# Two transformer blocks on one core: table work dealt by a rate over the feed-forward layers, its stores on GpSimd's queue, relu squares on ScalarE

## The chip, the cores and the metric

The kernel runs on one core of a Trainium2 chip. Its engines are TensorE (PE in the profile: matmuls and transposes), VectorE (DVE), ScalarE (ACT), GpSimd (POOL) and SyncE (SP, which here only issues DMAs). Each engine works through its own list of instructions in order and waits on semaphores for the others. The metric is the device time of one execution in microseconds (us), lower is better. A change of less than about 0.3% is not told from none here.

## The reference

The input is 256 tokens of 1024 features, in fp32. A first block of two layers and a second block of two layers follow one another; each ends in a feed-forward part of the same kind, so there are four of them:

```python
def squared_relu_mlp(h, w1, w2):
    a = jax.nn.relu(h @ w1)
    return (a * a) @ w2
# first block, layer l: x = x + rmsnorm(squared_relu_mlp(rmsnorm(x, g[4]), w_ff1[l], w_ff2[l]), g[5])
# second block, layer i: h = h + squared_relu_mlp_2(rms_norm(h, norm_ffn[i]), ffn_w_up[i], ffn_w_down[i])
```

w1 is 1024 x 4096, w2 4096 x 1024. The second layer of the second block has a state space mixer with weights of its own, of which much can be computed before the mixer's input is known:

```python
lam = lax.complex(a_re, a_im); dt = jnp.exp(log_dt)[..., None]
a_bar = jnp.exp(lam * dt)
b_bar = ((a_bar - 1.0) / lam)[..., None] * b_mat
# per direction r: bu = b_bar[r] u;  states by a scan with a_bar[r];  y = Re(c_mat[r] states)
# 64 groups of 16 features, 64 complex states each, both directions summed
```

## The kernel before

*Matrix products.* fp32 weights are split into two parts, and each product is three matmuls: high by high, low by high, high by low (`mm_a`, L217 to L219, and `mm_b`, L224 to L226). `Seg._load` (L33 on) loads a weight piece into a buffer `raw` (L42, issued by SP, four buffers), ACT makes the high part `whi` (L47, or L53 with a gain), DVE the low part `wlo` (L49 or L58). Ten buffers hold each of the two parts.

*The feed-forward part* (`mlp`, L275). The 4096 middle features are cut into eight chunks of 512. Chunks 0 and 1 are made token-major (`ff1_a`, then `out_a` with the transposes `fftp` of L337), chunks 2 to 7 feature-major (`ff1_b`, `out_b`). Behind the first product of chunk n comes the second product (`ff2`, tile `ffacc`) of chunk n - 2; at the end both last chunks follow with first all of one token half t = 0 and then t = 1. The middle result goes through `relu_sq`: ACT's relu out of the PSUM bank (L298), DVE's square in place (L299); `split` makes its parts `ah` on ACT (L292) and `al` on DVE (L293).

*The end of a feed-forward part.* `residual` (L178) takes the mean square by ACT (`junk`, L168), the factor `r` by DVE and POOL (L170, L171), and DVE adds into X (L200). `feat_half` transposes X on PE (`tp`, L140) and splits it again into `hh` (ACT, L143) and `hl` (DVE, L144) for the next part.

*The side work.* A generator `fill` is advanced one section by each `step(1)`: one at the start, then after each of the 4 column groups of a chunk and after each of the 4 row groups of `ff2`, so 1 + 6 x 8 = 49 steps; `step(100)` runs what is left. The first part (ff0) has `ssm_scalars` for it, 8 sections; the second (ff1) the tables of group blocks 0 to 7, the third (ffb0) those of 8 to 15 and then the loads of `ssm_prefetch`; the fourth (ffb1) has none. A layer's tables are 35 sections.

*A block of tables* (`ssm_tables`, L1354). `first(k)` loads `bc`, `pk`, `gb` and makes the complex products `er` and `gr`, each of four products, two on DVE and two (`cmt`) on POOL (`cmul`, L1149 to L1157), and POOL sets parts of `bm` to zero (L1378, L1379). `second(k)` follows one block later: twice four transposes of er on PE (`etp`, L1402) with a copy `eo` on ACT (L1403), then the lag products `klag` on PE (L1410, L1414), a copy `kl` on ACT (L1416) and a correction on DVE (L1417). What comes out is stored to DRAM tables: d_g, d_e (two halves), d_kl; at the end of the eight blocks d_ks is copied out of d_kl in two DMAs, and d_tt out of d_ks in eight (L1440). All of these DMAs are issued by SP, as the weight loads are.

*Order.* The order of the instructions on each engine is made by a scheduler before the run from the program's order, priorities and dependences; `first` stands at a lower priority. `order` rows below show what came of it.

Of the kernel before, what the change touches and what calls it, by code (L numbers as in the profile page):

```python
# [68 lines left out]
class Core:  # L69
# [204 lines left out]

    def mlp(self, pool, w1, gain, w2, done, perm=False, fill=None):  # L275

# [4 lines left out]
        rsq = []  # L281

        def step(n):
            for _ in range(n):
                if fill is not None:
                    next(fill, None)

# [7 lines left out]
        def relu_sq(ps, view=None):  # L295
            r = pool.tile([128, 512], F32, tag="relu", name="relu", bufs=2)
            o = r if view is None else view(r)
            nc.scalar.activation(out=o, in_=ps if view is None else ps.rearrange("p (f c j) -> p f c j", f=2, j=8), func=AF.Relu)  # L298
            nc.vector.tensor_tensor(out=r, in0=r, in1=r, op=ALU.mult)  # L299
            return r  # L300
# [82 lines left out]
        for ch in range(2, NCH):  # L383
            ps = ff1_b(ch, rest if ch == 2 else None)
            ff2([ch - 2], parts)
            parts[ch] = out_b(ps)
        step(100)
        ff2([NCH - 2, NCH - 1], parts)
# [739 lines left out]
class Ssm:  # L1128
# [225 lines left out]
    def ssm_tables(self, blocks, bc4, gain, d_rows, dmask):  # L1354
# [6 lines left out]
        with self.tc.tile_pool(name="tab", bufs=1, reuse_waits="tile") as pool:  # L1361

            def first(k):
# [24 lines left out]
                with self.low(90):  # L1388
                    gr = pool.tile([128, 4, 2, 8, 16], F32, tag="gr", name="gr", bufs=2)
                    self.cmul(pool, gr[:, :, 0], gr[:, :, 1], pj(16), pj(24), vi(cr), vi(ci), neg_i=True, tag="cte", second=G)  # L1390
                    A.activation(out=ci, in_=ci, func=AF.Copy, scale=-1.0)
                    nc.sync.dma_start(out=self.d_g[k], in_=gr.rearrange("p g r a b -> p (g r a b)"))
                yield k, bc, bm, er, gr

            def second(k, bc, bm, er, gr):
                cr, ci = bc[:, :, 2], bc[:, :, 3]
                for g2 in range(2):
# [5 lines left out]
                    A.activation(out=eo.rearrange("p g r n -> p (g r) n"), in_=ps, func=AF.Copy)  # L1403
                    nc.sync.dma_start(out=self.d_e[k, :, g2 * 512:g2 * 512 + 512], in_=eo.rearrange("p g r n -> p (g r n)"))
                    yield
# [11 lines left out]
                V.scalar_tensor_tensor(out=kl[:, 0:16], in0=dmask, scalar=d_rows[:, k:k + 1], in1=kl[:, 0:16], op0=MU, op1=AD)  # L1417
                nc.sync.dma_start(out=self.d_kl[k], in_=kl)

# [13 lines left out]
            ks = self.d_ks.rearrange("(a q) i n -> a q i n", q=4)  # L1433
            nc.sync.dma_start(out=ks[a0:a1, :, :, 112:240], in_=kl5[a0:a1, :, 0, :, 0:128])
            nc.sync.dma_start(out=ks[a0:a1, :, :, 0:112], in_=kl5[a0:a1, :, 1, :, 32:144])
            yield
            n = 4 * (a1 - a0)
            for r in range(8):
                src = bass.AP(self.d_ks.tensor, self.d_ks.offset + 4 * a0 * 16 * 240 + r * 16, [[240, 16], [3840, n], [1, 128]])
                nc.sync.dma_start(out=self.d_tt[r * 16:r * 16 + 16, 4 * a0:4 * a1, :], in_=src)  # L1440
            yield
# [278 lines left out]
def first_block(c, A):  # L1720
    tc, nc = c.tc, c.nc
    for l in range(2):
# [38 lines left out]
        with tc.tile_pool(name=f"ff{l}", bufs=1, reuse_waits="tile") as pool:  # L1761
            if l == 1:
                c.later.append(lambda: reorder(c))
            c.mlp(pool, A["w_ff1"][l], gc[2], A["w_ff2"][l], lambda t, a, q: c.residual(t, a, post, q), perm=l == 1,
                  fill=tables(c, A, range(8)) if l == 1 else c.ssm_scalars(A["ssm_a_re_2"], A["ssm_a_im_2"], A["ssm_log_dt_2"], c.sgn))

# [20 lines left out]
def second_block(c, A, out):  # L1787
# [5 lines left out]
    with tc.tile_pool(name="ffb0", bufs=1, reuse_waits="tile") as pool:  # L1793
        c.mlp(pool, A["ffn_w_up_2"][0], c.gcols[:, 8, :], A["ffn_w_down_2"][0], lambda t, a, q: c.residual(t, a, None, q, feat=False),
              fill=tables(c, A, range(8, 16), last=True))
    with tc.tile_pool(name="ssm", bufs=1, reuse_waits="tile") as pool:
# [84 lines left out]
```

## Time and profile before

| | us |
|---|---|
| median of three runs | 1510.27 (1508.42 to 1512.3) |
| the profiled execution | 1508.71 |
| its span, first to last instruction | 1506.9 |
| PE busy | 1426.2 |
| DVE busy | 1129.7 |
| ACT busy | 835.0 |
| POOL busy | 184.0 |

The mean granted TensorE clock is 0.979 of full speed. In the rows below a timeline line gives start and duration in us, engine, line, operation, output and inputs, and in brackets the idle time of the engine before it and what ended that; a line of a window gives its bounds, its length, then the busy time of PE, PEld (weight loads of PE), DVE, ACT and POOL with the number of instructions, the granted clock, the share of the DMA engines, and GB/s. SPq is SP's issue of a DMA. The four feed-forward parts lie at about 233.6 to 423.5 (ff0), 646.4 to 869.1 (ff1), 995.4 to 1208.8 (ffb0) and 1313.6 to 1497.0 (ffb1).

### The profile page before, as it was taken

The numbers are of one execution on the slowest core, as the hardware profiler recorded it, in microseconds if no ns is written. First come the engines' busy times: TensorE is split into PE (matmuls) and PEld (weight loads), VectorE is DVE, ScalarE is ACT, GpSimd is POOL, SyncE is SP. The second block draws the span as 40 slices with busy tenths as digits, with TensorE's granted clock in tenths as the row PEclk, the third lists the DMA queues.
The fourth block names the chain that finished last, engine by engine and source line by source line (L and its number), as shares of the span: only waits on it lengthen the run. The fifth ranks groups of instructions, "written<-read, shape, count | busy, mean of one in ns | idle before, by whom it ended". The sixth has DMA issues, their size and how long they took to land. (4 is left out here: it accounts for less than half of the span.)

```text
span 1506.9 us, 25499 instructions
## 1 busy us (share of the span) xinstructions
PE 1426.2 (95%) x9668; PEld 1239.6 (82%) x9668; DVE 1129.7 (75%) x2013; ACT 835.0 (55%) x1432; POOL 184.0 (12%) x206
## 2 busy tenths in 40 slices
PE   8999999999999999989899999999999968999997
PEld 8897888998789798869778877888879756889895
DVE  7986658997776866579995699899995587674651
ACT  7475546454464665556445667665454555564540
POOL 1241001000000000023440010123430000000000
PEclk9999999999999999999999999999999998999999
DMA  8464535475785455365768663347668887655640
GB/s 298 145 206 155 188 119 188 152 238 181 241 284 188 127 182 194 114 210 191 232 211 255 210 219 114 111 146 235 220 223 265 319 315 274 198 184 192 206 158 28
DMA packets 134034, 298.26 MB, mean 198 GB/s; under 512 B 16152, under 2 KB 36376, under 8 KB 133272
## 3 DMA queue, kind: packets, MB, share of 16 engines
q1 hardware_dynamic: 133624, 294.54, 58.9%
q0 software_dynamic: 288, 2.10, 0.4%
q8 instruction: 76, 1.25, 0.3%
q14 instruction: 46, 0.38, 0.1%
HBM read 270.15 MB, written 31.62 MB: 200 GB/s over the span
## 5 line engine op out<-in xcount | busy, mean ns | idle before, releaser
L58 DVE SCALAR_TENSOR_TENSOR wlo<-raw,gcols,whi 128x512 fp32r<-128x512 f32 (+1 forms) x456 | 356.7, 825 | 66.5 <-ACT whi L53 66.3
L53 ACT ACTIVATE whi<-raw,gcols 128x512 fp32r<-128x512 f32 (+1 forms) x456 | 316.7, 745 | 128.0 <-DMA raw<-in_w_ff 27.4
L49 DVE TENSOR_TENSOR wlo<-raw,whi 128x1024 fp32r<-128x1024 f32 x172 | 206.7, 1220 | 65.1 <-ACT whi L47 64.6
L47 ACT ACTIVATE whi<-raw 128x1024 fp32r<-128x1024 f32 x176 | 181.8, 1054 | 99.1 <-DMA raw<-in_ffn_w_down 28.6
L224 PE MATMUL ffps<-hh,whi 128*128 128x256 f32 x768 | 222.0, 289 | 0.2 <-ACT kl L1416 0.2
L226 PE MATMUL ffps<-hl,whi 128*128 128x256 f32 x768 | 219.6, 286 | 0.0
L225 PE MATMUL ffps<-hh,wlo 128*128 128x256 f32 x768 | 219.4, 286 | 0.0
L217 PE MATMUL ffacc<-whi,ah 128*128 128x512 f32 x512 | 206.1, 403 | 2.3 <-ACT whi L47 2.3
L218 PE MATMUL ffacc<-wlo,ah 128*128 128x512 f32 x512 | 203.5, 397 | 0.7 <-DVE wlo L49 0.7
L219 PE MATMUL ffacc<-whi,al 128*128 128x512 f32 x512 | 203.4, 397 | 0.0
L224 PEld LDWEIGHTS ffps<-hh,whi 128*128 128x128 f32 x768 | 148.2, 193 | 2.4 <-issue 1.4
L225 PEld LDWEIGHTS ffps<-hh,wlo 128*128 128x128 f32 x768 | 147.8, 192 | 0.5
L226 PEld LDWEIGHTS ffps<-hl,whi 128*128 128x128 f32 x768 | 147.6, 192 | 0.0
L217 PEld LDWEIGHTS ffacc<-whi,ah 128*128 128x128 f32 x512 | 97.3, 190 | 25.5 <-ACT whi L47 2.7
L218 PEld LDWEIGHTS ffacc<-wlo,ah 128*128 128x128 f32 x512 | 97.5, 190 | 22.7 <-DVE wlo L49 1.6
L219 PEld LDWEIGHTS ffacc<-whi,al 128*128 128x128 f32 x512 | 97.2, 190 | 23.0
L225 PE MATMUL pb<-hh,wlo 128*128 128x256 f32 x352 | 101.1, 289 | 2.9 <-DVE wlo L58 2.9
L224 PE MATMUL pb<-hh,whi 128*128 128x256 f32 x352 | 101.3, 290 | 2.2 <-ACT whi L53 2.2
L226 PE MATMUL pb<-hl,whi 128*128 128x256 f32 x352 | 100.8, 287 | 0.0
L171 POOL TENSOR_TENSOR r<-r,mhalf 128x1 f32<-128x1 f32 x32 | 24.7, 771 | 563.9 <-DVE r L170 557.2
L299 DVE TENSOR_TENSOR relu<-relu 128x512 f32<-128x512 f32 x64 | 45.7, 714 | 58.2 <-ACT relu L298 58.0
L298 ACT ACTIVATE relu<-ffps 128x512 f32<-128x512 f32 x64 | 43.9, 685 | 76.0 <-PE ffps L226 61.6
(481 smaller groups left out, 3001.7 us busy)
## 6 DMA issues: line engine op xcount, KB each, us to landing
raw<-in_w_ff SPq DMA_DIRECT2D x128, 512.0 KB, 4.6
raw<-in_ffn_w_up SPq DMA_DIRECT2D x64, 512.0 KB, 4.5
raw<-in_ffn_w_down SPq DMA_DIRECT2D x64, 512.0 KB, 4.4
raw<-in_w_mem_kv SPq DMA_DIRECT2D x32, 512.0 KB, 4.8
raw<-in_w_qkv SPq DMA_DIRECT2D x24, 512.0 KB, 4.9
raw<-in_attn_w_qkv SPq DMA_DIRECT2D x24, 512.0 KB, 4.7
raw<-in_w_in_ab SPq DMA_DIRECT2D x20, 512.0 KB, 5.1
raw<-in_w_mem_q SPq DMA_DIRECT2D x16, 512.0 KB, 5.1
```

The source lines that it names most:

```text
L47: nc.scalar.activation(out=hi, in_=src, func=AF.Copy)
L49: eng.tensor_tensor(out=lo, in0=src, in1=hi.bitcast(F32), op=ALU.subtract)
L53: nc.scalar.activation(out=hi[:, a], in_=src[:, a], func=AF.Copy, scale=g)
L58: nc.vector.scalar_tensor_tensor(out=lo[:, a], in0=src[:, a], scalar=g, in1=hi[:, a].bitcast(F32), op0=ALU.mult, op1=ALU.subtract)
L217: nc.tensor.matmul(o, xh, wh[:, s], start=first, stop=False)
L218: nc.tensor.matmul(o, xh, wl[:, s], start=False, stop=False)
L219: nc.tensor.matmul(o, xl, wh[:, s], start=False, stop=last)
L224: nc.tensor.matmul(out, wh, xh, start=first, stop=False)
L225: nc.tensor.matmul(out, wl, xh, start=False, stop=False)
L226: nc.tensor.matmul(out, wh, xl, start=False, stop=last)
L298: nc.scalar.activation(out=o, in_=ps if view is None else ps.rearrange("p (f c j) -> p f c j", f=2, j=8), func=AF.Relu)
L299: nc.vector.tensor_tensor(out=r, in0=r, in1=r, op=ALU.mult)
```

## The change

Three things. `step` collects a due count by a rate and advances the side work when it reaches one: 0.2 in ff0, 0.7 in ff1, 0.85 in ffb0. The stores of the tables (d_g, d_e, d_kl, d_ks, d_tt) are issued on GpSimd's queue. In the three parts with side work the square is an ACT instruction.

```diff
@@ -272,7 +272,8 @@
                     self.mm_b(ps[:, f, :], wh[:, c:c + 128], wl[:, c:c + 128], hh[:, :, kt, :], hl[:, :, kt, :], kt == 0, kt == KT - 1)
             consume(g, ps)
 
-    def mlp(self, pool, w1, gain, w2, done, perm=False, fill=None):
+    def mlp(self, pool, w1, gain, w2, done, perm=False, fill=None, rate=1.0):
+
 
         nc = self.nc
         hh, hl = self.hh, self.hl
@@ -280,10 +281,14 @@
         acc = []
         rsq = []
 
+        due = 0.0
+
         def step(n):
-            for _ in range(n):
-                if fill is not None:
-                    next(fill, None)
+            nonlocal due
+            due += n * rate
+            while fill is not None and due >= 1.0:
+                due -= 1.0
+                next(fill, None)
 
         def parts_tiles():
             return [pool.tile([128, 4, 2, 128], F32R, tag=nm, name=nm, bufs=3) for nm in ("ah", "al")]
@@ -296,7 +301,10 @@
             r = pool.tile([128, 512], F32, tag="relu", name="relu", bufs=2)
             o = r if view is None else view(r)
             nc.scalar.activation(out=o, in_=ps if view is None else ps.rearrange("p (f c j) -> p f c j", f=2, j=8), func=AF.Relu)
-            nc.vector.tensor_tensor(out=r, in0=r, in1=r, op=ALU.mult)
+            if fill is None:
+                nc.vector.tensor_tensor(out=r, in0=r, in1=r, op=ALU.mult)
+            else:
+                nc.scalar.activation(out=r, in_=r, func=AF.Square)
             return r
 
         def ff1_b(ch, mid=None):
@@ -384,7 +392,7 @@
             ps = ff1_b(ch, rest if ch == 2 else None)
             ff2([ch - 2], parts)
             parts[ch] = out_b(ps)
-        step(100)
+        step(1000)
         ff2([NCH - 2, NCH - 1], parts)
 
 TAIL = ((0, 0, 4), (1, 0, 2), (0, 4, 8), (1, 2, 8))
@@ -1389,7 +1397,7 @@
                     gr = pool.tile([128, 4, 2, 8, 16], F32, tag="gr", name="gr", bufs=2)
                     self.cmul(pool, gr[:, :, 0], gr[:, :, 1], pj(16), pj(24), vi(cr), vi(ci), neg_i=True, tag="cte", second=G)
                     A.activation(out=ci, in_=ci, func=AF.Copy, scale=-1.0)
-                    nc.sync.dma_start(out=self.d_g[k], in_=gr.rearrange("p g r a b -> p (g r a b)"))
+                    nc.gpsimd.dma_start(out=self.d_g[k], in_=gr.rearrange("p g r a b -> p (g r a b)"))
                 yield k, bc, bm, er, gr
 
             def second(k, bc, bm, er, gr):
@@ -1401,7 +1409,7 @@
                         for ri in range(2):
                             nc.tensor.transpose(ps[:, 2 * j + ri, :], er[:, ri, 2 * g2 + j].rearrange("p a b -> p (a b)"), self.ident)
                     A.activation(out=eo.rearrange("p g r n -> p (g r) n"), in_=ps, func=AF.Copy)
-                    nc.sync.dma_start(out=self.d_e[k, :, g2 * 512:g2 * 512 + 512], in_=eo.rearrange("p g r n -> p (g r n)"))
+                    nc.gpsimd.dma_start(out=self.d_e[k, :, g2 * 512:g2 * 512 + 512], in_=eo.rearrange("p g r n -> p (g r n)"))
                     yield
                 ps = self.ps.tile([128, 144], F32, tag="ps", name="klag")
                 for j in range(4):
@@ -1415,7 +1423,7 @@
                 kl = pool.tile([128, 144], F32, tag="kl", name="kl", bufs=2)
                 A.activation(out=kl, in_=ps, func=AF.Copy)
                 V.scalar_tensor_tensor(out=kl[:, 0:16], in0=dmask, scalar=d_rows[:, k:k + 1], in1=kl[:, 0:16], op0=MU, op1=AD)
-                nc.sync.dma_start(out=self.d_kl[k], in_=kl)
+                nc.gpsimd.dma_start(out=self.d_kl[k], in_=kl)
 
             last = None
             for k in list(blocks) + [None]:
@@ -1431,13 +1439,13 @@
             a0, a1 = blocks[0], blocks[-1] + 1
             kl5 = self.d_kl.rearrange("a (q d i) n -> a q d i n", q=4, d=2)
             ks = self.d_ks.rearrange("(a q) i n -> a q i n", q=4)
-            nc.sync.dma_start(out=ks[a0:a1, :, :, 112:240], in_=kl5[a0:a1, :, 0, :, 0:128])
-            nc.sync.dma_start(out=ks[a0:a1, :, :, 0:112], in_=kl5[a0:a1, :, 1, :, 32:144])
+            nc.gpsimd.dma_start(out=ks[a0:a1, :, :, 112:240], in_=kl5[a0:a1, :, 0, :, 0:128])
+            nc.gpsimd.dma_start(out=ks[a0:a1, :, :, 0:112], in_=kl5[a0:a1, :, 1, :, 32:144])
             yield
             n = 4 * (a1 - a0)
             for r in range(8):
                 src = bass.AP(self.d_ks.tensor, self.d_ks.offset + 4 * a0 * 16 * 240 + r * 16, [[240, 16], [3840, n], [1, 128]])
-                nc.sync.dma_start(out=self.d_tt[r * 16:r * 16 + 16, 4 * a0:4 * a1, :], in_=src)
+                nc.gpsimd.dma_start(out=self.d_tt[r * 16:r * 16 + 16, 4 * a0:4 * a1, :], in_=src)
             yield
 
     def ssm_prefetch(self):
@@ -1762,7 +1770,8 @@
             if l == 1:
                 c.later.append(lambda: reorder(c))
             c.mlp(pool, A["w_ff1"][l], gc[2], A["w_ff2"][l], lambda t, a, q: c.residual(t, a, post, q), perm=l == 1,
-                  fill=tables(c, A, range(8)) if l == 1 else c.ssm_scalars(A["ssm_a_re_2"], A["ssm_a_im_2"], A["ssm_log_dt_2"], c.sgn))
+                  fill=tables(c, A, range(8)) if l == 1 else c.ssm_scalars(A["ssm_a_re_2"], A["ssm_a_im_2"], A["ssm_log_dt_2"], c.sgn),
+                  rate=0.7 if l == 1 else 0.2)
 
 
 def reorder(c):
@@ -1792,7 +1801,7 @@
                A["attn_w_o_2"], A["cos"], A["sin"], lambda t, a: c.residual(t, a))
     with tc.tile_pool(name="ffb0", bufs=1, reuse_waits="tile") as pool:
         c.mlp(pool, A["ffn_w_up_2"][0], c.gcols[:, 8, :], A["ffn_w_down_2"][0], lambda t, a, q: c.residual(t, a, None, q, feat=False),
-              fill=tables(c, A, range(8, 16), last=True))
+              fill=tables(c, A, range(8, 16), last=True), rate=0.85)
     with tc.tile_pool(name="ssm", bufs=1, reuse_waits="tile") as pool:
         c.ssm(pool, X, A["ssm_w_glu_2"])
     c.pre_pool.__exit__(None, None, None)
```

Lines of the changed kernel stand 5 to 9 further down than before's (L1418 is L1426, L1392 is L1400, L1404 is L1412).

SP, in the middle of ff1. Before:

```order
L1418 DMA d_kl<-kl 128x144
L1369 DMA pk<-d_p 128x136
L1392 DMA d_g<-gr 128x1024
L42 DMA raw<-in_w_ff 128x2x512
L1404 DMA d_e<-eo 128x512
L42 DMA raw<-in_w_ff 128x2x512 x2
L1404 DMA d_e<-eo 128x512
L42 DMA raw<-in_w_ff 128x2x512
L1367 DMA bc<-in_ssm_bc 128x256
```

After, in the middle of ff1:

```order
L1379 DMA gb<-in_ssm_g 128x64
L42 DMA raw<-in_w_ff 128x2x512
L1375 DMA bc<-in_ssm_bc 128x256
L42 DMA raw<-in_w_ff 128x1024
L1377 DMA pk<-d_p 128x136
L42 DMA raw<-in_w_ff 128x1024
L1379 DMA gb<-in_ssm_g 128x64
L42 DMA raw<-in_w_ff 128x1024 x2
L42 DMA raw<-in_w_ff 128x2x512 x3
```

The stores d_kl, d_g and d_e have left the weight loads (raw); the small loads of a block (bc, pk, gb) are still among them.

POOL, from the last table products of ff1 (cmt) to the norm factors r of the residual at its end. Before:

```order
L1149 TENSOR_TENSOR cmt<-pk,bb 128x512
L1150 TENSOR_TENSOR cmt_8476<-pk,bb 128x512
L1149 TENSOR_TENSOR cmt<-pk,bc 128x512
L1150 TENSOR_TENSOR cmt_8510<-pk,bc 128x512
L1378 MEMSET bm 64x8x16
L1379 MEMSET bm 64x8x16
L171 TENSOR_TENSOR r<-r,mhalf 128x1 x4
```

POOL after, the last block's products:

```order
L1157 TENSOR_TENSOR cmt<-pk,bb 128x512
L1158 TENSOR_TENSOR cmt_8775<-pk,bb 128x512
L1412 DMA d_e<-eo 128x512 x2
L1157 TENSOR_TENSOR cmt<-pk,bc 128x512
L1158 TENSOR_TENSOR cmt_8820<-pk,bc 128x512
L1386 MEMSET bm 64x8x16
L1387 MEMSET bm 64x8x16
```

The products of er (pk,bb) and of gr (pk,bc) of one block now have a d_e pair of the block before between them. POOL after, directly behind these rows, up to r:

```order
L1426 DMA d_kl<-kl 128x144
L1400 DMA d_g<-gr 128x1024
L1412 DMA d_e<-eo 128x512 x2
L1426 DMA d_kl<-kl 128x144
L1412 DMA d_e<-eo 128x512 x2
L1426 DMA d_kl<-kl 128x144
L1442 DMA d_ks<-d_kl 512x1x128
L1443 DMA d_ks<-d_kl 512x1x112
L1448 DMA d_tt<-d_ks 16x32x128 x8
L171 TENSOR_TENSOR r<-r,mhalf 128x1 x4
```

The norm factors r stand behind the last d_kl, both d_ks and eight d_tt.

PE, at the end of ff1, where X of the first token half is transposed (tp) beside the last second products (ffacc), behind which the next part's products (acc) begin. Before:

```order
L217 MATMUL ffacc_7442<-whi,ah 128x512
L218 MATMUL ffacc_7442<-wlo,ah 128x512
L219 MATMUL ffacc_7442<-whi,al 128x512
L140 MATMUL tp<-ident,X 128x128 x8
L217 MATMUL ffacc_7441<-whi,ah 128x512
L218 MATMUL ffacc_7441<-wlo,ah 128x512
```

After:

```order
L217 MATMUL ffacc_7415<-whi,ah 128x512
L218 MATMUL ffacc_7415<-wlo,ah 128x512
L219 MATMUL ffacc_7415<-whi,al 128x512
L140 MATMUL tp<-ident,X 128x128 x8
L217 MATMUL acc_9398<-whi,hh 128x512
L218 MATMUL acc_9398<-wlo,hh 128x512
```

Before, 24 ffacc matmuls follow the eight transposes; in the changed kernel none does.

## Rows read from the trace of the kernel before

**Rows 1.** The page's busy line: engine, busy us, share of the span, instructions.

```profile
PE 1426.2 (95%) x9668; PEld 1239.6 (82%) x9668; DVE 1129.7 (75%) x2013; ACT 835.0 (55%) x1432; POOL 184.0 (12%) x206
```

**Rows 2.** Windows of ff1, ffb0 and ffb1; columns as told above.

```profile
646.40:869.10 222.70, 205.78 (x1410) 178.57 (x1410) 180.71 (x277) 122.99 (x206) 55.56 (x49) 0.96 0.67 218
995.40:1208.80 213.40, 202.81 (x1402) 175.35 (x1400) 172.69 (x266) 106.69 (x186) 52.44 (x49) 0.98 0.71 240
1313.60:1497.00 183.40, 183.40 (x1082) 161.38 (x1080) 98.73 (x125) 85.82 (x122) 0.99 (x1) 1.00 0.50 161
```

**Rows 3.** Timeline of PE: an etp and a klag group and what follows.

```profile
734.51 0.60 PE L1402 MATMUL etp<-ident,er 128*128 128x128 f32 x4
734.86 0.48 PE L217 MATMUL ffacc<-whi,ah 128*128 128x512 f32 x1
...
741.15 0.33 PE L1410 MATMUL klag<-bc,bm 128*32 128x16 f32 x15
...
741.88 0.39 PE L224 MATMUL ffps<-hh,whi 128*128 128x256 f32 x1
```

**Rows 4.** Waits of PE in ff1, then ffb0: us in total, times, longest.

```profile
PE etp L1402 <- ACT eo L1403: 5.6, 2, 3.3
...
PE etp L1402 <- ACT eo L1403: 5.5, 2, 3.3
```

**Rows 5.** Windows of 3 us behind PE's longest gap of ff1.

```profile
678.00:681.00 3.00, 2.76 (x13) 2.79 (x14) 3.00 (x5) 2.79 (x4) 0.00 (x0) 0.50 0.20 70
681.00:684.00 3.00, 3.00 (x23) 3.00 (x22) 2.48 (x5) 2.50 (x6) 2.20 (x1) 0.81 0.76 253
```

**Rows 6.** Window of ff1 in which tables are made.

```profile
682.00:800.00 118.00, 108.22 (x880) 95.15 (x883) 112.39 (x174) 65.31 (x115) 45.68 (x40) 0.96 0.66 219
```

**Rows 7.** Timeline of SP and ACT before one of etp's gaps.

```profile
742.67 0.32 SPq L1392 DMA_DIRECT2D d_g<-gr  x1
...
744.28 0.46 SPq L1404 DMA_DIRECT2D d_e<-eo  x1
...
748.28 1.33 ACT L53 ACTIVATE whi<-raw,gcols 128x512 fp32r<-128x512 f32 x2 [5.95 <-DMA raw<-in_w_ff]
```

**Rows 8.** Timeline of POOL and PE at ff0's end.

```profile
412.12 0.77 POOL L429 DMA_DIRECT2D mh<-d_mem  x1 [21.91 <-ACT whi L53]
412.88 0.55 POOL L429 DMA_DIRECT2D ml<-d_mem  x1
...
415.16 1.71 PE L140 MATMUL tp<-ident,X 128*128 128x128 f32 x8 [3.35 <-DVE X L200]
```

**Rows 9.** Squares of ff1 (count, busy us, mean ns), and ACT's wait for them.

```profile
L299 DVE TENSOR_TENSOR relu<-relu 128x512 f32<-128x512 f32 x16 | 11.9, 744 | 16.9 <-ACT relu L298 16.7
...
ACT ah L292 <- DVE relu L299: 12.9, 9, 3.6
```

**Rows 10.** Timeline of ACT, DVE and PE at PE's longest gap of ff1.

```profile
674.27 0.63 ACT L168 ACTIVATE junk<-X 128x512 f32<-128x512 f32 x1 [1.28 <-DMA X<-d_x]
...
675.66 0.57 ACT L298 ACTIVATE relu<-ffps 128x512 f32<-128x512 f32 x1
...
677.41 0.68 DVE L299 TENSOR_TENSOR relu<-relu 128x512 f32<-128x512 f32 x1
...
678.24 1.09 PE L337 MATMUL fftp<-ident,relu 128*128 128x128 f32 x4 [6.87 <-DVE relu L299]
```

**Rows 11.** Timeline of SP at ff1's last stores, and of PE's last ffacc.

```profile
808.20 0.38 SPq L1418 DMA_DIRECT2D d_kl<-kl  x1
...
817.28 5.55 SPq L1440 DMA_DIRECT2D d_tt<-d_ks  x8
...
868.52 0.39 PE L218 MATMUL ffacc<-wlo,ah 128*128 128x512 f32 x1
868.75 0.39 PE L219 MATMUL ffacc<-whi,al 128*128 128x512 f32 x1
```

**Rows 12.** Timeline of DVE: a product of er beside POOL's.

```profile
658.85 1.55 DVE L1151 TENSOR_TENSOR er<-pk,bb 128x512 f32<-128x512 f32 x1
```

## The prediction

> **What bounds the kernel now.** I began with the page's busy line: of a span of 1506.9 us TensorE (PE) is busy 1426.2 and VectorE (DVE) 1129.7 [rows 1]. So PE bounds the whole, and a change to other engines can only give back PE's idle time and the half-speed stretches that follow it. Then I cut three of the four feed-forward layers (MLPs) out by windows [rows 2]: ff1 222.7 us, ffb0 213.4, ffb1 183.4. The last carries no side work and PE never idles in it, so 183.4 is what an MLP costs when everything is hidden. ff1 and ffb0 carry the state space tables, 39 and 30 us more.
>
> Part of that is PE work that stays. Four transposes (etp) take 0.35 us of PE's time, the distance from their start to the next matmul's, and a klag group 0.73 (741.15 to 741.88) [rows 3]. A block has two etp groups and one klag group: 2 x 0.35 + 0.73 = 1.43, taken as 1.5; eight blocks 12 us. Without stalls ff1 and ffb0 would take 183.4 + 12 = 195.4. The excess is 27.3 in ff1 and 18.0 in ffb0, 45.3 together. That is what there is to win.
>
> Next the waits of PE in both MLPs. In ff1 the longest is 6.87 us at 678.24, for the square of a relu [rows 10]; 5.6 in two gaps are for a copy of etp, and in ffb0 5.5 in two, the longest 3.3 [rows 4]. After a gap the clock falls: behind the 6.87 us the granted clock is 0.50 of full speed (the 1.2 GHz level) in 678 to 681 and 0.81 in 681 to 684 [rows 5]. In those two slices PE does the work of 1.5 + 2.4 us in 6, so a gap costs about 2 us more; I use 2.0 behind this longest gap and, as an estimate, 1.7 behind the shorter ones.
>
> Why the gaps arise: in 682 to 800, while tables are made, DVE is busy 112.4 of 118 us [rows 6], in ffb1 98.7 of 183.4 [rows 2]. The tables are packed into the first 35 of 49 steps, and there DVE is full. At 748.28 ScalarE (ACT) stands 5.95 us for a weight tile, because SyncE (SP) issues it behind two table stores (742.67, 744.28) [rows 7], and the copy eo, for which PE's etp waits, comes behind that on ACT. So it is dense DVE work and SP's mixed order that make these gaps.
>
> **The change part by part.** *The rates.* ff1 0.7 and ffb0 0.85 spread 35 sections over 49 and 41 of the 49 steps. DVE's work in ff1 is 180.7 us [rows 2]; over some 209 us instead of the first 150 its mean share falls from 0.95 to about 0.8. ff0's eight sections of scalars at 0.2 go to every fifth step; at its end a stall of 3.35 [rows 8] has nothing to do with them: 0.
>
> *Squares.* A DVE square is 744 ns in the mean, 16 per such MLP: 11.9 us off DVE [rows 9]. On ACT no square is shown; its nearest row, the relu of the same size, is 0.57 [rows 10], so about 9.5 us more for ACT, which is busy 123.0 of 222.7 [rows 2]: cover is there. Bounds of the edit: in 16 places ACT's turn changes from relu, wait for DVE, ah to relu, square, ah; it may gain the 12.9 us that ah waited for DVE [rows 9], or cost 16 x 0.57 = 9 where ACT is late. Neither is on PE's path now, except in one place, so 0. The exception is the gap that ends at 678.24: relu ended at 676.2, DVE's square started only at 677.41 [rows 10]. ACT had stood for the reload of X until 674.27 [rows 10]. With the square on ACT it ends about 675.7 and PE starts at 675.8: 4.4 of 6.87 stay, with the half clock of 2.0 behind.
>
> *Stores.* 16 d_g, 32 d_e, 16 d_kl and the d_ks, d_tt leave SP, where a d_g takes 0.32 us [rows 7] and eight d_tt 5.55 [rows 11]. Weight loads no longer queue behind a store that waits for DVE or ACT. What they cost on GpSimd (POOL) is not shown before, except by two other DMAs at 412: 0.77 and 0.55 us of its time [rows 8]. I take 0.66 for a 128-row store, and 0.66 x (5.55 / 8) / 0.32 = 1.4 for a d_tt of 512 rows; bounds 0.55 (no growth) to 0.77 x 4 = 3.1 (by rows). POOL has the room: 55.6 of 222.7 busy [rows 2], and in each MLP 32 such stores, two d_ks and eight d_tt add 32 x 0.66 + 10 x 1.4 = 35.
>
> The added waits: a store on POOL waits for DVE or ACT there, and the products cmt, the memsets and r stand behind it. r is the norm's factor of the residual (row L171). In ff1 it stands behind the last d_kl, two d_ks and eight d_tt. The last klag is 108 ffacc matmuls before the MLP's last, 25 us at the 0.23 from one's start to the next's [rows 11]. d_kl follows some 2.5 us later (my estimate: a copy on ACT and a correction on DVE, each in its turn). From d_kl's issue to the first d_tt SP needed 817.28 - 808.20 = 9.1 [rows 11]. So the d_tt start about 13.5 us before the end and take 8 x 1.4 = 11; r follows some 2 before the end, and its X (2 x 0.7 on DVE) is ready about at the end. PE's transposes of X stand behind the last ffacc in the new order (before they stood 24 ffacc ahead of it), so the chain tp, hh, hl is uncovered: hh is a copy of 128x512 on ACT, 0.57 as the relu [rows 10], hl a DVE instruction of that size, 0.74 [rows 9], tp two groups of four, 0.7 [rows 3]: 2.0, which I take, between 0 (hidden after all) and 2.7 (a weight split of 0.7 ahead of hl). In ffb0 the residual makes no such transposes, and r is behind nothing long: 0.
>
> *The stalls left.* I expect one to survive in each MLP, of the etp kind: 3.3 + 1.7 of half clock = 5.0. Bounds: none, or three.
>
> The sum: ff1 195.4 + 4.4 + 2.0 + 2.0 + 5.0 = 208.8, 13.9 less. ffb0 195.4 + 5.0 = 200.4, 13.0 less. Everything else 0, give or take 4, as the state space layer reads its tables in another order. 26.9 off the profiled execution's 1508.7 is 1481.8; the median of the runs lies 1.6 higher, so 1483.
>
> A rule that speaks against the stores: the Trainium skill ("DMA: Bandwidth & Descriptors", Issuing engines are not separate DMA queues) says that issuing from several engines saves only the issuer's own time, usually small beside the transfer. By that alone the stores would give 32 x 0.32 + 5.55 = 16 us of SP's time and nothing of PE's; a stall more would stay in each MLP, 1483 + 10 = 1493. The trace disagrees in what matters here: SP's price was not its 0.32 us but the waiting store ahead of a weight load [rows 7].
>
> **Rivals.** *Slower: POOL's in-order queue ties DVE to PE.* The next block's cmt stand behind the last block's two d_e, which wait for eo, which waits for PE's etp; DVE needs cmt for er and gr, and PE needs er for the next etp. If PE must wait in each of 14 blocks as it does now for etp, 14 x (3.3 + 1.7) = 70 is paid against the 45.3 removed: 1508.7 + 25 = about 1534. It decides from nine such stalls on. For it: POOL already sets DVE back, an er product takes 1.55 beside POOL's reads [rows 12], where another product of two tensors of that size takes 0.68 [rows 10]. Against it: blocks are now some 25 us apart and POOL's own part of a block is 7.
>
> *The tail of ff1.* If a d_tt costs 2.5 to 3.1, the eight of them take 9 to 14 us longer than above and PE stands as long at the transposes, with 1.7 of clock to regain: 1483 + 11 to 15, 1494 to 1498. For it: at 412 r stood behind two POOL DMAs and PE waited 3.35 [rows 8]. Against it: on SP a d_tt is only twice a d_g [rows 11]. The Trainium skill ("SBUF — State Buffer", Summary: rules for kernel authors) would have stores on GpSimd starve while DVE runs in its two-port modes, and keep them on SP or ACT; by it this tail is the likelier, at its upper end, 1498. It names copies, casts and tensor_scalar for these modes, and the DVE work here is nearly all of two tensors; no row before shows a store on POOL beside busy DVE.
>
> *All stalls vanish.* DVE at 0.8 feeds everything and ff1 keeps only its first gap and the tail: 26.9 + 10.0 = 36.9, 1473. For it: ffb1, with DVE at 0.54, has no gap [rows 2]. Against it: etp still waits for a copy that ACT makes in turn.
>
> *No effect.* The stalls come from the round trip DVE, PE, ACT of a block and not from density: 1508 to 1511. Against it: of ff1's 16 etp groups only two made PE wait for eo [rows 4].
>
> **How the numbers follow.** The forecast 0.58, its own range 1475 to 1493 (a stall fewer or two more, tail 0 to 2.7, the state space layer 4 either way, not all at once); all stalls vanish 0.12; the tail 0.13; no effect 0.05; slower 0.12. The first three cases are faster by over 0.3% (below 1505.7; about what a measurement of this kernel can tell from no change): 0.83. Within 0.3%: 0.05. Slower: 0.12. The range must reach the vanished stalls and the tail, 1471, and toward the slower case until two in ten are left out: 1507.
>
> **What would show it.** Right: windows of ff1 and ffb0 near 209 and 200; DVE's busy share there about 0.8 and even; PE's wait for the relu between 4 and 5 us, now put down to ACT; SP rows of weight loads with no store between. Wrong: PE waits for etp or klag in more than three blocks, POOL's cmt waiting for d_e, a gap of over 5 us at ff1's end before the transposes of X, or a POOL store over 2 us.

## The result and the profile after

The changed kernel takes 1491.25 us (median of four runs, 1484.9 to 1491.94) against 1509.35 of four runs of the kernel before: a ratio of 0.9869 (0.9837 to 0.9900). The forecast was 1483, 8 us too low. All stage readings below are made on profiled executions, as the forecast's sum was: the span fell from 1506.9 to 1489.3, by 17.6. The granted clock is 0.981 in the mean (0.979 before), so the clock as a whole is not the cause.

The span cut into stages, each from TensorE's (PE's) timeline, from the first instruction of one feed-forward part (MLP) to the end of its last second-product matmul (ffacc), and what lies between:

| stage | before | after | change |
|---|---|---|---|
| head, up to ff0 | 233.6 | 232.0 | -1.7 |
| ff0 | 189.8 | 184.0 | -5.8 |
| ff0 to ff1 | 223.0 | 225.3 | +2.3 |
| ff1 | 222.5 | 205.6 | -16.9 |
| ff1 to ffb0 (attention's front) | 126.5 | 138.0 | +11.5 |
| ffb0 | 213.1 | 197.0 | -16.1 |
| ffb0 to ffb1 (state space layer) | 105.1 | 114.2 | +9.1 |
| ffb1 | 183.2 | 183.2 | 0 |

The MLPs gave 38.8 us; the two stretches behind those with tables took 20.6 of them back. In the windows of the changed kernel (columns as in [rows 2]) the first and third lines, ff1 and ffb0, answer to [rows 2], the second and fourth are the stretches behind them, the fifth answers to [rows 6], and the last two are the slices behind the new gap:

```profile
641.30:846.90 205.60, 200.30 (x1401) 174.14 (x1399) 170.14 (x256) 128.39 (x217) 81.60 (x90) 0.98 0.72 239
846.90:984.90 138.00, 123.65 (x649) 100.15 (x649) 118.13 (x271) 90.97 (x187) 13.33 (x14) 0.96 0.41 130
984.90:1182.00 197.10, 197.10 (x1401) 171.69 (x1399) 158.01 (x239) 112.53 (x197) 80.45 (x88) 1.00 0.74 258
1182.00:1296.10 114.10, 87.63 (x1161) 69.62 (x1161) 79.74 (x118) 59.04 (x97) 4.55 (x10) 0.90 0.70 247
682.00:800.00 118.00, 118.00 (x915) 104.56 (x914) 112.57 (x173) 76.43 (x130) 59.88 (x63) 1.00 0.70 237
856.00:859.00 3.00, 2.40 (x9) 2.07 (x10) 2.97 (x6) 2.41 (x8) 0.32 (x1) 0.50 0.33 127
859.00:862.00 3.00, 3.00 (x10) 2.22 (x9) 2.07 (x6) 1.23 (x4) 0.78 (x2) 0.63 0.00 0
```

The two stretches in the kernel before:

```profile
869.10:995.40 126.30, 121.17 (x641) 97.31 (x640) 114.61 (x267) 88.78 (x181) 12.91 (x13) 1.00 0.46 146
1208.80:1313.60 104.80, 86.61 (x1161) 70.01 (x1161) 76.29 (x107) 56.27 (x91) 4.21 (x7) 0.92 0.74 266
```

In ffb0 PE is busy for the whole 197.1 us at a clock of 1.00: no wait is left. In ff1 one of note is left, of which more below. In 682 to 800 PE does not idle either (it was busy 108.22 at 0.96 in [rows 6]). VectorE (DVE) is as busy there as it was, 112.57 against 112.39 of 118. This is the first surprise: PE's stalls went, and DVE is as full as before. In this window it makes the er products of seven blocks in either kernel; for the nine squares that left it makes 57 low parts of weights where it made 48. So the rates did not thin out DVE's table work there. What they moved is PE's side of it: here the last instruction of a block's er ends 22 to 24 us before its transposes start, where before it was 6 to 14.

Three gaps of PE in the changed kernel (start, duration, instruction, idle time before it and what ended it): the one left in ff1, in front of a relu's transposes, and the two where time went back, at the end of ff1 and at the head of the state space layer:

```profile
671.27 1.11 PE L345 MATMUL fftp<-ident,relu 128*128 128x128 f32 x4 [4.78 <-ACT relu L307]
856.60 1.94 PE L140 MATMUL tp<-ident,X 128*128 128x128 f32 x8 [9.56 <-issue]
1196.14 1.97 PE L1529 MATMUL utp<-ident,xp 128*128 128x128 f32 x8 [14.04 <-ACT xp L1515]
```

The second gap is named "issue", so the profile names no releaser. DVE's timeline of the changed kernel shows what the transposes of X stood behind:

```profile
838.06 5.61 DVE L58 SCALAR_TENSOR_TENSOR wlo<-raw,gcols,whi 128x512 fp32r<-128x512 f32 x8 [0.40 <-ACT whi L53]
...
847.46 4.06 DVE L58 SCALAR_TENSOR_TENSOR wlo<-raw,gcols,whi 128x512 fp32r<-128x512 f32 x6 [1.28 <-ACT whi L53]
851.81 0.20 DVE L650 TENSOR_SCALAR qkg<-qkg 128x64 f32<-128x64 f32 x1 [0.29 <-DMA qkg<-in_attn_q_gain]
...
854.41 0.29 DVE L662 TENSOR_TENSOR lp<-lv 128x128 f32<-128x128 f32 x1 [0.84 <-DMA lv<-in_attn_lambda]
...
855.56 0.15 DVE L194 TENSOR_TENSOR r<-r,rsq 128x1 f32<-128x1 f32 x1
855.75 1.41 DVE L200 SCALAR_TENSOR_TENSOR X<-y,r,X 128x512 f32<-128x512 f32 x2
```

GpSimd (POOL) had made the norm's factor r long before:

```profile
832.51 5.09 POOL L1448 DMA_DIRECT2D d_tt<-d_ks  x8 [3.17 <-DMA d_ks<-d_kl]
837.81 0.56 POOL L171 TENSOR_TENSOR r<-r,mhalf 128x1 f32<-128x1 f32 x1 [0.20 <-DVE r L170]
```

r is there at 838.4, X starts at 855.75, 17 us later: in DVE's new order the residual stands behind sixteen low parts of weights (838.06 to 851.5) and then eighteen small instructions that make the attention's constants. SyncE (SP) issues the loads of these constants (qkg to lv) only at 847.65 to 849.11. Each takes 0.15 to 0.3 us, all of them 3.9 (851.81 to 855.7). PE's gap lies at 847.0 to 856.6, so the low parts fill as much of it as the constants do. Behind the gap the clock is 0.50, the 1.2 GHz level, and then 0.63.

At the state space layer, ScalarE's (ACT's) timeline in the changed kernel:

```profile
1190.80 0.63 ACT L1573 ACTIVATE rt<-rho 128x512 f32<-128x512 f32 x1 [7.16 <-DMA rho<-d_rho]
1191.45 4.63 ACT L1515 ACTIVATE xp<-X,r 32x256 f32<-32x256 f32 x10
```

SP in the changed kernel:

```profile
1181.43 1.37 SPq L1472 DMA_DIRECT2D e<-d_e  x3
1182.85 0.43 SPq L1494 DMA_DIRECT2D rho<-d_rho  x1
```

ACT stands 7.16 us for the load rho, which SP issues behind three table loads, and ten xp, which the transposes utp wait for, queue behind. Before, the same instruction stood 0.80 us, behind the ten xp and not ahead of them, and PE 6.20 in front of utp. The load is not the whole gap: utp waits for DVE's share of xp too, and in e1, e2, e10, e11 and e12 below that wait ends last and the gap is still 11.1 to 11.2.

### The profile page after: what moved, and what is told of

It is laid out like the page before. It is cut to its first block, busy times and chain, and to the rows that moved or that the text cites. A ratio compares the mean times of both kernels' runs of the same rounds, so it can differ in the third digit from the quotient of the medians.

```text
span 1489.3 us, 25554 instructions
## 1 busy us (share of the span) xinstructions
PE 1416.3 (95%) x9668; PEld 1232.1 (83%) x9668; DVE 1103.0 (74%) x1965; ACT 859.6 (58%) x1480; POOL 238.4 (16%) x290
## 4 chain that ended last, share of the span: by engine, by line
PE 56%; DMA 4%; DVE 4%; issue 1%; ACT 1%; POOL 0%; SPq 0%; DVEq 0%; POOLq 0%; ACTq 0%
PE ffacc L217 6%; PE ffacc L219 6%; PE ffacc L218 6%; PE ffps L224 5%; PE ffps L226 5%; PE ffps L225 5%; PE pacc L217 2%; PE pacc L219 2%; PE pacc L218 2%; PE pb L224 1%; PE pb L225 1%; PE pb L226 1%; PE ffps L219 1%; PE ffps L217 1%; PE ffps L218 1%
## 5 line engine op out<-in xcount | busy, mean ns | idle before, releaser
L53 ACT ACTIVATE whi<-raw,gcols 128x512 fp32r<-128x512 f32 (+1 forms) x456 | 316.9, 745 | 110.1 <-PE pb L226 17.6
L225 PEld LDWEIGHTS pb<-hh,wlo 128*128 128x128 f32 x352 | 68.0, 193 | 3.8 <-DVE wlo L58 3.7
```

The lines of the kernel that those rows point to most:

```text
L53: nc.scalar.activation(out=hi[:, a], in_=src[:, a], func=AF.Copy, scale=g)
L225: nc.tensor.matmul(out, wl, xh, start=False, stop=False)
```

## The experiments

Stage lengths of every run, in us, from the profiles, as in the table above; the medians' ratios to the kernel before, measured anew beside each set of runs, with 95% intervals, stand with each experiment.

| run | ff0 | ff1 | ff1 to ffb0 | ffb0 | ffb0 to ffb1 | span |
|---|---|---|---|---|---|---|
| before | 189.8 | 222.5 | 126.5 | 213.1 | 105.1 | 1506.9 |
| changed | 184.0 | 205.6 | 138.0 | 197.0 | 114.2 | 1489.3 |
| e1 tail on SP | 184.0 | 207.2 | 139.3 | 198.8 | 111.1 | 1490.0 |
| e2 rates only | 184.3 | 217.2 | 138.7 | 203.3 | 110.9 | 1504.9 |
| e3 stores only | 186.8 | 223.4 | 137.4 | 209.1 | 112.3 | 1521.9 |
| e4 squares only | 184.0 | 215.1 | 126.1 | 203.3 | 107.3 | 1486.5 |
| e5 residual first | 184.0 | 206.6 | 139.2 | 197.4 | 109.1 | 1486.7 |
| e6 squares, rate 0.9 | 184.1 | 226.1 | 126.8 | 204.8 | 103.8 | 1494.6 |
| e7 e6, block stores on POOL | 184.1 | 221.2 | 126.8 | 204.6 | 105.6 | 1490.0 |
| e8 rate 1, tail on SP | 184.0 | 219.9 | 127.0 | 205.3 | 107.7 | 1490.8 |
| e9 two more buffers | 188.7 | 219.2 | 127.0 | 219.5 | 106.6 | 1512.8 |
| e10 constants later | 184.0 | 206.4 | 140.4 | 200.1 | 110.0 | 1491.1 |
| e11 e10, all stores on SP | 184.0 | 207.2 | 141.8 | 197.0 | 108.5 | 1486.3 |
| e12 splits first | 184.0 | 209.3 | 146.5 | 197.0 | 111.6 | 1498.4 |

**e2, e3, e4: each part alone, on the kernel before.**

```diff
 e2:  the rates 0.2, 0.7 and 0.85 as in the change, nothing else
 e3:  all five stores
-nc.sync.dma_start(out=self.d_...
+nc.gpsimd.dma_start(out=self.d_...
 e4:  relu_sq, in the parts with side work
-nc.vector.tensor_tensor(out=r, in0=r, in1=r, op=ALU.mult)
+nc.scalar.activation(out=r, in_=r, func=AF.Square)
```

> The kernel before with the rates alone (stores on SP, squares on DVE). Theory A (a full DVE makes the stalls of the feed-forward parts; spreading frees it; no price at the two ends): most of the 39 us that the feed-forward parts lost in the changed kernel are gained, 1472 to 1480. Theory B (SP's mixed order makes the stalls, the rates bring the two new waits): the stalls stay and 10 to 20 us are added, 1515 to 1530.

> The kernel before with the stores alone on POOL (rates 1, squares on DVE). Theory A: DVE is as full as before, so the stalls stay, and the two waits at the ends are added: 1515 to 1530. Theory B: the stalls go with the stores and nothing is added, 1470 to 1480.

> The kernel before with the squares alone on ACT (rates 1, stores on SP). Theory A: DVE's share in the dense stretch falls from 0.95 to about 0.87, which takes a part of the stalls and 2 us of the first gap: 1490 to 1505. Theory B: DVE is not the cause, 1506 to 1511.

Measured: e2 1508.95 (ratio 1.0014, 1.0000 to 1.0027), e3 1522.92 (1.0110, 1.0090 to 1.0130), e4 1488.47 (0.9878, 0.9860 to 0.9897). For e2 neither theory's range was met; e3 fell in that of theory A, e4 just below that of its theory A. The squares alone give all that the whole change gives; the rates alone give nothing; the stores alone cost 16 us (the span 15.0). The squares and the rates each make ff1 and ffb0 shorter, to about 215 to 217 and 203, and neither alone to 206 and 197. But e2 pays 12.2 and 5.8 us in the two stretches behind, and e4 pays -0.4 and 2.2. (For ff1, e6 to e8 below limit what e4 shows.)

Of e3's loss 10.9 us lie behind ff1, with the same displaced residual. DVE in e3, at the end of ff1:

```profile
874.34 0.19 DVE L647 TENSOR_SCALAR qkg<-qkg 128x64 f32<-128x64 f32 x1 [0.91 <-DMA qkg<-in_attn_q_gain]
...
877.52 1.42 DVE L200 SCALAR_TENSOR_TENSOR X<-y,r,X 128x512 f32<-128x512 f32 x2
```

POOL's r was done there at 861.1, and sixteen low parts of weights stand ahead of the constants there too. In e4 X comes first and the constants stand behind even the second half of X, as in the kernel before. DVE in e4:

```profile
847.69 1.41 DVE L200 SCALAR_TENSOR_TENSOR X<-y,r,X 128x512 f32<-128x512 f32 x2
861.23 1.41 DVE L200 SCALAR_TENSOR_TENSOR X<-y,r,X 128x512 f32<-128x512 f32 x2
862.55 0.18 DVE L650 TENSOR_SCALAR qkg<-qkg 128x64 f32<-128x64 f32 x1
```

What the squares do beside the 12 us they take off DVE shows in what ACT waits for. Waits of ACT in 640 to 1215 (total, times, longest), first in the kernel before, then in e2:

```profile
ACT ah L292 <- DVE relu L299: 30.6, 19, 4.8
...
ACT ah L297 <- DVE relu L304: 45.8, 20, 7.5
```

In e4 and in the changed kernel there is none. A relu that comes back squared from DVE holds up ACT's whole queue, in which the weight parts and eo stand behind ah; with the square on ACT this round trip is gone. I did not part it from the 12 us by a run, and e2 speaks against taking it for the whole cause: there the wait grew to 45.8 us, and ff1 and ffb0 are 5.3 and 9.8 shorter all the same.

**e1: the changed kernel with only the end of the tables (d_ks, d_tt) back on SP.**

```diff
-nc.gpsimd.dma_start(out=ks[a0:a1, ...
+nc.sync.dma_start(out=ks[a0:a1, ...
-nc.gpsimd.dma_start(out=self.d_tt[...
+nc.sync.dma_start(out=self.d_tt[...
```

> The changed kernel, but the d_ks and d_tt copies are issued by SP again. Theory A: the two new waits of the changed kernel, 9.6 us at the transposes of X behind ff1 and 14.0 at the head of the state space layer, come from d_ks and d_tt standing on POOL, which puts the residual's X behind other work in the order. Then both fall back to what they were, some 20 us less with the half clock: 1491 - 20 = 1471. Theory B: they come from the rates, which let the tables end later; then nothing changes, 1488 to 1492.

1487.76 (0.9879, 0.9861 to 0.9898), not told from the changed kernel and at the edge of theory B's range. The gap at tp went, yet the stretch behind ff1 stayed long (139.3): the wait came up further down. PE in e1:

```profile
868.71 1.22 PE L217 MATMUL acc<-whi,hh 128*128 128x512 f32 x2 [6.18 <-ACT whi L53]
872.48 0.80 PE L218 MATMUL acc<-wlo,hh 128*128 128x512 f32 x1 [2.55 <-DVE wlo L58]
```

and ACT in e1, the exponential of the constants ahead of the weight parts:

```profile
867.84 0.20 ACT L665 ACTIVATE ls<-ls 128x2 f32<-128x2 f32 x1 [6.65 <-DVE ls L664]
867.95 5.01 ACT L53 ACTIVATE whi<-raw,gcols 128x512 fp32r<-128x512 f32 x8
```

**e5, e10, e12: three ways to move what stands at the end of ff1 in the order.** e5 gives the residuals a higher priority, e10 (on e1) the constants a lower one, e12 (the rates and squares, all stores on SP) the weight parts a higher one.

```diff
 e5:  in ff1 and ffb0
+with c.tc.high_priority(offset=400):
+    c.residual(t, a, post, q)
 e10: around sg, lv, lp, ls and nlam
+with self.low(400):
 e12: in place of that, around the attention's weights
+with self.low(-400):
     wh, wl = seg.get(kt)
```

> The changed kernel with the residual behind ff1 and ffb0 at a higher priority for the scheduler (d_ks, d_tt stay on POOL, the rates stay). Theory P, place: the two new waits are made by where the scheduler puts X, behind the constants of the next stage on DVE and ACT; put first, the 9.6 us behind ff1 fall to 2 or 3 (the second token half still stands behind the constants) and the head of the state space layer from 14.0 to about 8: 1491 - 8 to 12 = 1478 to 1483. Theory Q, late tables: the copies at the tables' end cost the time themselves, whatever the order of X: 1488 to 1493, or more since d_tt now stands behind r.

> The run with d_ks and d_tt on SP (rates, squares, blocks' stores on POOL), and in the attention behind ff1 the constants of lambda at a lower priority for the scheduler, so that ACT's exponential of them no longer stands ahead of 20 weight splits. Theory P, place: the wait for the splits, 6.2 and 2.6 us of PE, goes with its half clock, the stretch from ff1 to ffb0 falls from 139 to about 128: 1475 to 1480. Theory Q: late tables cost this stretch by something else and the wait comes back in another place: 1485 to 1490.

> Rates and squares of the changed kernel, all table stores on SP, and in the attention behind ff1 the weight pieces (load and split) at a higher priority for the scheduler than the norm of the keys. In the runs with rate 0.7 ACT splits 8 or 9 pieces of 512 columns in the 30 us behind ff1, in those whose stretch to ffb0 is 126 or 127 us 20 to 23. Theory P, place: the pieces stand behind the norm of the keys only by the order; put first, that stretch falls from 139 to 142 to about 128: 1491 - 12 = 1475 to 1481. Theory Q: with the tables so late DVE and SP have no room to prepare the pieces, whatever the order; the wait comes back or moves into ff1: 1486 to 1493.

1490.2 (0.9890, 0.9872 to 0.9909), 1491.55 (0.9895, 0.9876 to 0.9914) and 1497.17 (0.9924, 0.9909 to 0.9940). None met its theory P; e5 fell in the range of theory Q, e10 and e12 above it. None got the 126 us back: the stretch took 139.2, 140.4 and 146.5. The wait took other places each time. In e5, PE stood 4.0 us at tp and 4.7 at the transposes tq of the attention; e10 and e12 on PE:

```profile
872.12 0.79 PE L218 MATMUL acc<-wlo,hh 128*128 128x512 f32 x1 [9.17 <-DVE wlo L58]
```

```profile
901.91 1.94 PE L739 MATMUL tq<-ident,z 128*128 128x128 f32 x8 [11.57 <-DVE z L733]
```

So what stands ahead of X at the gap is shown, and that changing the order there is not enough. The added time is waiting of PE and slow clock behind it: PE is idle 4 to 6 us of the stretch, at a granted clock of 0.99 to 1.00, in the runs with 126 to 127 us, and 12 to 20 us, at 0.92 to 0.96, in the long ones. What makes the stretch 11 to 20 us longer in all variants at rates of 0.7 and 0.85 stays open. A trace of it: in the 30 us behind ff1 ACT makes 20 to 22 weight parts in the runs with 126 to 127 us and 8 to 11 in most of the long ones, but 13 in the changed kernel and 19 in e5, so this alone does not settle it.

e5 also tells on the state space layer. There ACT makes its ten xp ahead of rt again, and PE's gap at utp falls from 14.04 to 6.06, as in the kernel before; but its stretch is 109.1, still 4 us longer than before's 105.1.

**e6, e7, e8: the squares with denser tables,** to keep ff1's gain without the price behind it.

```diff
 e6:  e4 with rate 0.2, 0.9, 1.0
 e7:  e6 with d_g, d_e, d_kl on nc.gpsimd
 e8:  e7 with rate 0.2, 1.0, 1.0
```

> Squares on ACT, rates 0.9 in ff1 and 1.0 in ffb0 (0.2 in ff0), all stores on SP; the order behind ff1 is then that of the kernel before. Theory P: the stretch behind ff1 is 126 as with the squares alone and ff1 gains a little from the lower rate (215 to about 211): 1478 to 1486. Theory Q: the copies end 20 us later than with the squares alone and cost a part of their 12 us: 1488 to 1494.

> As the run with squares and 0.9, and the blocks' stores (d_g, d_e, d_kl) on POOL, d_ks and d_tt on SP. If the stores among the weight loads cost PE anything once the squares are on ACT: 3 to 8 us below that run, 1472 to 1480. If not: the same as that run within 2 us.

> Squares on ACT, rates 1.0 throughout, the blocks' stores on POOL, d_ks and d_tt on SP. If density still matters when the squares are on ACT: slower than the run with 0.9 by 3 to 8 us and as the squares alone or a few us under it, 1480 to 1488. If only the squares count: within 2 us of the run with 0.9.

1494.2 (0.9918, 0.9899 to 0.9937), 1493.67 (0.9917, 0.9895 to 0.9940), 1493.74 (0.9923, 0.9905 to 0.9942): all three 5 to 6 us slower than e1 and e4. None reached its faster case; e7 and e8 are the same as e6, as their second cases had it. The stretches behind are short (126.8 to 127.0), ff1 is long again (219.9 to 226.1). In e8 the block stores are on POOL and the stretch is not long, so in e3 it is d_ks and d_tt there, or the squares' absence, that makes it so.

These runs limit what e4 shows. With the squares on ACT and rates of 0.9 or 1, ffb0 is 8 to 10 us shorter than before in all four runs and ff0 5.7 to 5.8, but ff1 is 7.4 shorter in e4, 1.3 and 2.6 in e7 and e8, and 3.6 longer in e6. So in ff1 the squares alone are worth no sure amount.

e6 also tells on density. A window of e6 within ff1, and a wait of PE in its ff1:

```profile
690.00:812.00 122.00, 107.76 (x883) 95.04 (x882) 104.54 (x165) 73.13 (x129) 40.63 (x36) 0.96 0.70 227
...
PE ffps L224 <- ACT eo L1411: 8.1, 2, 4.2
```

DVE is busy 0.86 there, less than the 0.95 of the changed kernel, and PE loses 14 us where that loses none. PE waits for table work (etp, klag, or what stands behind their copies) in ff1 in e2, e4, e6, e7 and e8 (6.3 to 14.3 us); in the changed kernel, e1, e5, e10, e11 and e12, with squares and rates of 0.7 and 0.85 together, it does so for 0.9 us at most. Why 0.9 is worse in ff1 than 1.0 (226.1 and 221.2 against 215.1 and 219.9) I cannot say.

**e9: two more raw buffers on the kernel before,** as a rival to both: if ACT's waits for weights [rows 7] make the stalls, more buffers should remove them whatever the stores do.

```diff
# and, around ff1 and ffb0, a pool rawx of two such buffers
-src = c.raw.tile([128, h, w], ...
+src = (c.rawx if c.rawx is not None and c.nload % 3 == 2 else c.raw).tile([128, h, w], ...
```

> The kernel before with two more buffers for raw weight pieces in ff1 and ffb0 (six in place of four); no part of the change. Theory R, raw buffers: PE's stalls in these parts come along a ring: DVE's low parts are late behind table products, so a raw buffer is late free, so SP loads the next piece late, so ACT waits for it with eo and relu behind it, and PE waits for those. Two more buffers cut the ring: ff1 222 to about 203, ffb0 213 to about 199, in all 1470 to 1480. Theory D, DVE is full: more buffers do not help, only less DVE work at a time: 1502 to 1510.

1514.67 (1.0048, 1.0030 to 1.0067), slower than either theory had it. In e9, the stretch of [rows 6]:

```profile
682.00:800.00 118.00, 107.87 (x887) 94.31 (x886) 115.94 (x176) 64.69 (x116) 42.24 (x38) 0.96 0.68 222
```

PE is no busier than in [rows 6] (108.22), and in ffb0 a PE wait for the copy eo remains:

```profile
1135.42 1.11 PE L1404 MATMUL etp<-ident,er 128*128 128x128 f32 x4 [5.33 <-ACT eo L1405]
```

ACT's waits for weight loads of ff1, first in the kernel before, then in e9 (total, times, longest):

```profile
ACT whi L53 <- DMA raw<-in_w_ff: 21.3, 8, 5.9
ACT whi L47 <- DMA raw<-in_w_ff: 9.3, 12, 1.9
...
ACT whi L48 <- DMA raw<-in_w_ff: 1.3, 1, 1.3
ACT whi L54 <- DMA raw<-in_w_ff: 1.1, 1, 1.1
```

The wait of 5.95 in [rows 7] is gone. With it went PE's waits for eo in ff1, but those for klag grew from 3.4 us to 10.1; ff1 is 3.3 us shorter and ffb0 6.4 longer. So weights that come earlier move PE's waits and do not remove them.

**e11: e10 with all stores on SP,** that is the rates and squares without the stores.

```diff
-nc.gpsimd.dma_start(out=self.d_...
+nc.sync.dma_start(out=self.d_...
```

> As the run with the constants at a lower priority, but all table stores on SP (rates 0.2, 0.7, 0.85 and the squares on ACT). If the blocks' stores among the weight loads cost PE something: ff1 212 or more, ffb0 202 or more, 5 to 12 us slower than that run. If the rates and the squares do it: within 2 us of it, ff1 about 207 and ffb0 199.

1490.75 (0.9890, 0.9869 to 0.9910), the same as e10, as expected if the rates and the squares do it. In e11:

```profile
638.60:845.80 207.20, 200.41 (x1410) 174.35 (x1409) 171.97 (x261) 128.86 (x220) 60.96 (x49) 0.98 0.73 233
987.50:1184.60 197.10, 197.10 (x1401) 171.70 (x1400) 156.13 (x243) 112.40 (x200) 54.50 (x48) 1.00 0.76 252
```

With every table store among the weight loads on SP, both MLPs are as free of waits for table work as in the changed kernel. The stores' move contributes nothing to the gain.

## Why the prediction was right in its time and wrong in a cause

*ff1 and ffb0: right in place and nearly in size.* Leaving the 2.0 of the tail out, which falls behind the window, the forecast was 206.8 and 200.4; measured 205.6 and 197.0. The base of 195.4 without stalls holds: ffb0 is 1.6 above it. The first gap was to shrink to 4.4 and is 4.78, and its releaser is now ACT's relu as predicted. But that the size fits is luck: in e2, with the square still on DVE, the same gap is 4.8, and with the square on ACT it ran from 3.6 (e4) to 7.2 (e8). The stalls of 5.0 that I let survive in each MLP did not: the rival "all stalls vanish" was right there.

*Squares: the step that failed.* "Neither is on PE's path now, except in one place, so 0." The first gap's 2.5 apart, the sum had nothing for them. Alone (e4) they shorten ffb0 by 9.8, ff0 by 5.8 and ff1 by 7.4, the last not in e6 to e8; together with the rates they are the whole of the gain in the MLPs (e11). I saw the 12.9 us for which ACT waited for DVE's square [rows 9], and set it at nothing because PE did not wait for that instruction itself; but what PE waits for stands behind it on ACT. That this wait is the way by which the squares help is an argument; the 11.9 us less of DVE's work is the rival, and no run parts the two.

*Stores: wrong in cause.* "It is dense DVE work and SP's mixed order that make these gaps." e11 keeps SP's mixed order and has only the relu's gap, and e9 takes ACT's waits for weights from 30.6 us to 2.4 in ff1 and leaves PE idle 14.5 us there, where it was 16.9. [rows 7] showed a wait that is real and whose removal gave next to nothing. Here the Trainium skill ("DMA: Bandwidth & Descriptors", Issuing engines are not separate DMA queues), which grants the issuer's own time and no more, stood nearer to the result than my reading did: e10 and e11, which differ in the issuer of the block stores alone, are 0.8 us apart. Even the 1493 worked out beside it was nearer to 1491.25, though by terms that came out otherwise. On the kernel before, though, moving all stores cost 16 us by the order that came of it (e3).

*Dense DVE work: half right.* The rates matter for the last stalls (215.1 and 203.3 in e4 against 207.2 and 197.0 in e11). But the forecast's "busy share about 0.8 and even" did not come: the share in 682 to 800 stayed 0.95. Over all of ff1 it is 0.83 (170.14 of 205.6), but there it was 0.81 before (180.71 of 222.7); the forecast had set the share of a stretch against the mean of a whole part. Over ff1 DVE does 10.6 us less, about the squares. Whether this, the order on ACT, or the longer lead of er over its transposes does it, no run parts.

*The tail of ff1: the mis-sized term.* Forecast 2.0, bounds 0 to 2.7; the gap is 9.56 and its stretch 11.5 longer. A gap of over 5 us there was one of the prediction's own signs of being wrong. I had named the place and the wrong cause: the eight d_tt take 0.63 us of POOL's time each (1.4 taken), so r was ready 8.5 us before ff1's end, not 2; what the sum left out is DVE's order between r and X, the sixteen low parts of weights and the constants. The tail's rival, 11 to 15 us through dear d_tt, gave about the right size by a mechanism that did not happen. e1, with d_ks and d_tt off POOL, is not shorter.

*The state space layer and ff0.* 0, give or take 4, became +9.1: 7.8 of it is the longer gap at utp, at which ACT stood at rt for a load that SP issues among the table loads. e5 took that gap back and 5.1 us of the stretch; all variants with rates of 0.7 and 0.85 pay there (108.5 to 114.2), the others less (103.8 to 107.7), save e3 (112.3). ff0's 0 became -5.8: the stall in [rows 8] went in every variant with the rates or the squares. I had written that it "has nothing to do with" the rates.

*The slower rival did not happen.* POOL did wait for eo with its stores, but no wait of PE came of it. (The blocks' transposes came 13 to 19 us apart in ff1, not 25.) In the changed kernel's ff1, the store (count, busy time, mean ns, idle before and releasers):

```profile
L1412 POOL DMA_DIRECT2D d_e<-eo x16 | 9.0, 561 | 31.5 <-ACT eo L1411 25.5 <-DVE bb L1161 4.6 <-DMA raw<-in_w_ff 1.2
```

25.5 us of waiting on POOL, and no wait of PE for etp or klag in either MLP. So the time was close by luck, because two errors met: 38.8 us won in the MLPs where 28.9 were forecast, and 20.6 lost behind them where 2.0 were.

## What to carry to other kernels

Where an engine works in order, the wait to look for is not only the one that the bounding engine names, but any wait on the engine that feeds it, and its size does not tell its worth: here 30.6 us of ACT standing for DVE's squares went with an 18 us gain (that it caused the gain is not shown), and 30.6 us of ACT waiting for weight loads in ff1, all but taken away, with a loss of 8. Undo each part of a change apart before crediting any: here one part (the squares) carries the gain, one (the rates) moves about as much behind the stage as it takes out of it, and one (the stores) costs 16 us alone and nothing beside the other two. And when side work is spread to a stage's end, read what then stands at that boundary, the next stage's weight parts and small late-loaded constants too: 20.6 of 38.8 us were lost there.

## What the runs showed of the hardware

A store issued by POOL beside a DVE that is busy 112.57 of 118 us costs no more than the two DMAs of [rows 8] did (0.77 and 0.55). From the tile views of the changed kernel (duration in ns, least, middle and most; first and last start):

```profile
L1412 POOL DMA_DIRECT2D d_e<-eo x32: 539/546/599, 695.0 to 1135.2; - x32
...
L1448 POOL DMA_DIRECT2D d_tt<-d_ks x16: 630/630/652, 832.5 to 1159.0; - x16
```

A d_tt of four times the rows takes 0.63, hardly more than a d_e; DVE is busy only 1.54 us of the 5.1 in which the first eight are issued. The Trainium skill ("SBUF — State Buffer", Summary: rules for kernel authors) warns of GpSimd's stores starving beside DVE's two-port modes; with the work of two tensors that DVE does here, the d_e took 0.60 us at most. And the square on ACT takes 625 ns, where DVE's took 744 in the kernel before [rows 9]:

```profile
L307 ACT ACTIVATE relu<-relu 128x512 f32<-128x512 f32 x16 | 10.0, 625 | 0.1
```
